# The preparation of an RWKV-7 recurrence put in a fixed order on three engines, its masks moved next to the Gram products, and Gram and bonus products merged into longer runs

## The chip, the cores and the metric

The kernel runs on one core of one Trainium2 chip. The core has five engines, each with its own queue of instructions that it works off strictly in the order in which they stand: TensorE (PE, matrix products and transposes into PSUM), VectorE (DVE), ScalarE (ACT), GpSimd (POOL) and SyncE (SP, which only issues DMA here; ACT issues some too). An instruction that has to wait holds up everything behind it in its own queue, and nothing else. The metric is the device time of one execution in microseconds.

## The reference

One layer of a decoder trunk over 1024 tokens of width 1024, in float32. Three branches read the same normalised input: an RWKV-7 recurrence, stick-breaking attention, and cross-attention into 256 memory tokens. They are gated, merged and projected; a feed-forward block with a causal convolution follows.

```python
h = rms_norm(x, norm1_g);  proj = h @ w_in
p_rwkv, p_sb, q_mem, gate_logits = split(proj)
# RWKV-7, 8 heads of 64
p = p + (shift(p) - p) * mu;  r, k, v, wl, al, gl = split(p)
decay = exp(-exp(-softplus(-(w0 + tanh(wl) @ w2)) - 0.5))
a = sigmoid(a0 + al @ a2);  g = sigmoid(gl) @ g2
kk = k * k_k;  kk = kk / max(norm(kk), 1e-12)       # per head
k = k * (1 + (a - 1) * k_a)
S_t = S * decay_t - (S kk_t) (kk_t a_t)^T + v_t k_t^T;   y_t = S_t r_t
y = (groupnorm(y) + bonus) * g,   bonus = sum(r * k * r_k) * v
# merge, then
x = x + sum_b(sigmoid(G_b) * (branch_b @ w_branch_b)) @ w_out
x = x + (silu(gate) * val) @ w_down,   gate, val = causal_conv3(rms_norm(x) @ w_up)
```

## The kernel before

Every large product is done as three products of rounded halves: a weight tile is loaded (`wr`), ACT copies it to a rounded high part (`wh`, L81), POOL subtracts to get the low part (`wl`, L82), and `mm3` issues high by high, high by low and low by high. A 1024-deep projection of 128 output columns and all 1024 tokens has eight steps of six matmuls over 512 tokens and fills two PSUM banks; the V projection of the stick-breaking attention (`sb_v`) fills four at once. PSUM has eight banks here: four of tag `mm` for projections, four of tag `g` for everything else.

The recurrence is computed in chunks of 64 tokens. `rwkv_prep(p, ...)`, called for p = 0 to 3 with two heads each, makes all that it needs: sigmoids of the low-rank products, the decay scan (L330), the norm of k by heads (`head_ss`, L333 to L337), the gate, the transposed v, kk and b (L369, L370), and for each half h of the tokens a pair of factors `bk`, `ra` (`chain(h)`, L379 to L382), their Gram products (`gram(h, f)`, f for a quarter: eight products of 128 by 128, then two masks L396 on DVE from PSUM to SBUF, then stores), a decayed copy on POOL (`decayed`, L408) and its transposes (`turned`). The bonus (L428 to L430) is made between chain(0) and gram(0).

`weave` interleaves that generator with `pump`, the stream of projections: after each `yield` of the preparation one step of the pump follows, six matmuls. So the PE order is written out by hand by the number of yields. While `self.pin` is set, `pinned` keeps PE's matmuls and transposes in program order; the instructions of the other engines are ordered by a scheduler from its own costs, with those in the preparation given priority (`high_priority`). A projection of the recurrence is finished by `shifted`: two products with a row scale (L246, which free the PSUM banks), a shifted copy on ACT (L247) and a final sum (L249). Behind the four preparations come the stick-breaking attention (`sb_attn`), the memory attention, `stage2` with the recurrence itself, and later the up phase and the down phase. Between them run on DVE the inverses of the triangular systems (L462, L464), driven by `pump`, and the differences of V rows (L681) which wait for loads of `vsd`.

In the down phase a step is 12 matmuls over one `draw` load: SP loads activations (`actd`, L1666) and weights (L1669), ACT copies both (L1676, L1677), DVE and POOL subtract (L1678, L1679). At the way into it the last tiles of the up phase are still convolved (L1473 on ACT, L1474, L1475 and L1481 on DVE) and combined (L1490), and ACT issues their stores to `actd` (L1495 to L1500).

## Time and profile before

| what | value |
| --- | --- |
| median of 3 runs | 1835.45 us (1835.12 to 1835.46) |
| the profiled execution | 1834.23 us |
| its span | 1832.5 us |
| mean clock granted to PE | 0.997 of full speed |
| preparations, about | 40 to 286 us |
| stick-breaking attention, about | 310 to 610 us |
| the way into the down phase | 1605 to 1630 us |

The span runs from the first to the last instruction of the profiled execution; its own time is a little longer, as it holds what lies around. In a waits view a row names the engine and line that waited, what released it, the total, the number and the longest wait in us. In a timeline a row has its start, its length, the line, the shapes, how many alike were joined (x), and in brackets the idle time before and what ended it. In a stretch of windows each engine has its busy time and, in brackets, its instructions, followed by the granted clock, the busy share of the DMA engines and their GB/s.

### The profile page before, as it was taken

The page shows a single profiled execution, that of the slowest core. Times are in us where ns is not written, and L with a number is a line of the kernel's source. Part 1 is how long each engine was busy: PE and PEld are TensorE (multiplying, and loading weights), DVE is VectorE, ACT ScalarE, POOL GpSimd, SP SyncE. Part 2 cuts the span into 40 slices and gives each one's busy share as a digit, 9 for nine tenths or more (in the row PEclk, how much of TensorE's full clock was granted, in tenths as well). Part 3 has the DMA queues.
Part 4 walks back from the last instruction along what each step waited for, and adds up shares of the span by engine and source line. Part 5 has one row for each costly group of instructions (what it writes and reads, how often), then busy time and mean ns, then how long its engine had stood idle before and what let it go on. Part 6 is the DMA issues. An engine that isn't in the chain of part 4 may idle for free.

```text
span 1832.5 us, 27438 instructions
## 1 busy us (share of the span) xinstructions
PE 1783.7 (97%) x10468; PEld 1442.8 (79%) x10468; DVE 1185.4 (65%) x1659; ACT 881.4 (48%) x1665; POOL 770.6 (42%) x441
## 2 busy tenths in 40 slices
PE   8999999999999999999899999989999999999999
PEld 6777778778788887787777878868888888878877
DVE  5657664988987514333534792597776777794596
ACT  5443342564666636534456533454444444444333
POOL 2322343232222452122233350476767767635454
PEclk9999999999999999999999999999999999999999
DMA  4155466111112342467665563323332323395475
GB/s 181 58 172 184 161 195 198 50 41 52 56 50 81 111 143 55 167 212 256 229 230 185 194 220 104 127 68 106 113 106 87 119 95 116 115 334 206 138 248 189
DMA packets 120614, 263.39 MB, mean 144 GB/s; under 512 B 28314, under 2 KB 40858, under 8 KB 120355
## 3 DMA queue, kind: packets, MB, share of 16 engines
q1 hardware_dynamic: 82722, 194.76, 32.3%
q10 hardware_dynamic: 33984, 54.27, 8.1%
q0 software_dynamic: 3776, 12.62, 2.2%
q8 instruction: 82, 1.34, 0.3%
q14 instruction: 50, 0.40, 0.1%
HBM read 180.04 MB, written 81.53 MB: 143 GB/s over the span
## 4 chain that ended last, share of the span: by engine, by line
PE 81%; DVE 10%; issue 4%; ACT 2%; POOL 2%; DMA 1%; ACTq 0%; SPq 0%; DVEq 0%; POOLq 0%
PE mm L113 65%; PE g L113 13%; PE g L106 3%; POOL dw L1679 1%; DVE at L854 1%; DVE it L462 1%; DVE qk L379 1%; DVE qk L381 1%; DVE inst L464 1%; DVE BT L1318 1%; DVE mg L1232 0%; DVE qk L817 0%; DMA at<-scr 0%; DVE g L1474 0%; ACT wh L81 0%
## 5 line engine op out<-in xcount | busy, mean ns | idle before, releaser
L82 POOL TENSOR_TENSOR wl<-wr,wh 128x1024 fp32r<-128x1024 f32 x77 | 196.5, 2552 | 475.0 <-ACT wh L81 464.1
L113 PE MATMUL mm<-xhi,wh 128*128 128x512 f32 x784 | 263.3, 416 | 10.1 <-ACT xhi L182 8.1
L113 PE MATMUL mm<-xlo,wh 128*128 128x512 f32 x784 | 244.7, 393 | 0.3 <-DVE xlo L183 0.3
L113 PE MATMUL mm<-xhi,wl 128*128 128x512 f32 x784 | 243.2, 392 | 0.7 <-POOL wl L82 0.7
L113 PEld LDWEIGHTS mm<-xhi,wl 128*128 128x128 f32 x784 | 147.6, 188 | 34.3 <-POOL wl L82 1.6
L113 PEld LDWEIGHTS mm<-xlo,wh 128*128 128x128 f32 x784 | 147.9, 189 | 33.8 <-DVE xlo L183 1.0
L113 PEld LDWEIGHTS mm<-xhi,wh 128*128 128x128 f32 x784 | 137.2, 190 | 40.1 <-issue 9.1
L81 ACT ACTIVATE wh<-wr 128x1024 fp32r<-128x1024 f32 x77 | 81.4, 1057 | 143.6 <-PE mm L113 87.3
L113 PE MATMUL mm<-dw,da 128*128 128x512 f32 x528 | 121.5, 390 | 2.2 <-DVE da L1678 2.0
L113 PEld LDWEIGHTS mm<-dw,da 128*128 128x128 f32 x528 | 98.8, 188 | 24.3 <-DVE da L1678 3.4
L113 PE MATMUL mm<-BT,l 128*128 128x512 f32 x504 | 117.7, 389 | 0.0
L1679 POOL TENSOR_TENSOR dw<-draw,dw 128x512 fp32r<-128x512 f32 x55 | 81.5, 1488 | 83.3 <-ACT dw L1677 83.2
L113 PE MATMUL mm<-BT,wh 128*128 128x512 f32 x352 | 109.2, 390 | 2.8 <-DVE BT L1318 2.8
L854 DVE TENSOR_TENSOR_SCAN at<-at,at 128x128 f32<-128x128 f32 (+3 forms) x64 | 93.3, 1459 | 26.6 <-ACT at L848 26.4
L113 PEld LDWEIGHTS mm<-BT,l 128*128 128x128 f32 x504 | 94.6, 188 | 19.6
L113 PE MATMUL mm<-B,wh 128*128 128x512 f32 x352 | 108.6, 390 | 1.5 <-DVE p L1508 1.5
L1678 DVE TENSOR_TENSOR da<-draw,da 128x512 fp32r<-128x512 f32 x77 | 65.7, 863 | 57.6 <-ACT da L1676 57.1
L113 PE MATMUL g<-dw,da 128*128 128x512 f32 x396 | 90.9, 390 | 2.1 <-POOL dw L1679 1.1
L1409 POOL TENSOR_TENSOR l<-it,l 128x1024 fp32r<-128x1024 f32 x21 | 51.6, 2459 | 95.5 <-ACT l L1408 95.5
L113 PEld LDWEIGHTS g<-dw,da 128*128 128x128 f32 x396 | 74.2, 188 | 18.3 <-ACT dw L1677 1.4
L1676 ACT ACTIVATE da<-draw 128x512 fp32r<-128x512 f32 x77 | 48.3, 629 | 83.6 <-PE mm L113 38.1
L756 DVE TENSOR_TENSOR w<-w,rbc 128x1024 f32<-128x1024 f32 x24 | 49.8, 2074 | 56.8 <-ACT w L755 55.0
(329 smaller groups left out, 3989.9 us busy)
## 6 DMA issues: line engine op xcount, KB each, us to landing
wr<-in_w_in_dram SPq DMA_DIRECT2D x50, 512.0 KB, 3.7
draw<-actd SPq DMA_DIRECT2D x77, 256.0 KB, 4.3
at<-scr SPq DMA_DIRECT2D x28, 512.0 KB, 6.1
draw<-in_w_down_dram SPq DMA_DIRECT2D x55, 256.0 KB, 4.9
rw<-in_w_up_dram SPq DMA_DIRECT2D x22, 512.0 KB, 3.5
actd<-gall ACTq DMA_DIRECT2D x44, 256.0 KB, 3.4
gsd<-w ACTq DMA_DIRECT2D x20, 512.0 KB, 2.8
wr<-in_w_up_dram SPq DMA_DIRECT2D x20, 512.0 KB, 3.7
```

The costliest lines, as they stand in the source:

```text
L81: self.nc.scalar.activation(hi, raw, AF.Copy)
L82: self.nc.gpsimd.tensor_tensor(lo, raw, hi.bitcast(F32), ALU.subtract)
L106: self.pinned(self.nc.tensor.transpose(out, in_, self.ident[:n, :n]))
L113: self.pinned(self.nc.tensor.matmul(*a, **k))
L379: nc.vector.tensor_tensor(bk4[q, :, first ^ h2], self.c8(x[q, hs]), self.c8(Q[q, hs]), ALU.mult)
L381: nc.vector.scalar_tensor_tensor(ra4[:, :, 1, 1:64], self.c8(P[:, hs])[:, :, 0:63], -1.0, self.c8(kk[:, hs])[:, :, 1:64], ALU.mult, ALU.mult)
L756: nc.vector.tensor_tensor(g, g, self.rbc, ALU.mult)
L854: self.pinned(nc.vector.tensor_tensor_scan(sn[:, :W][:, ::-1], sn[:, :W][:, ::-1], self.smask[:, 1024 - W :][:, ::-1], 1.0, ALU.mult, ALU. ...
L1409: keep(eng.tensor_tensor(lo, src, hi.bitcast(F32), ALU.subtract))
L1676: self.pinned(nc.scalar.activation(A[:, 0], a, AF.Copy))
L1678: self.pinned(nc.vector.tensor_tensor(A[:, 1], a, A[:, 0].bitcast(F32), ALU.subtract))
L1679: nc.gpsimd.tensor_tensor(Wt[:, 1], w, Wt[:, 0].bitcast(F32), ALU.subtract)
```

## The change

The number of instructions on each engine stays as it was, and what is computed too. Five things differ.

1. `pinned` now covers DVE, ACT and POOL instructions of the preparation, of `shifted` and, while `pin_split` is set, of the weight splits. It also adds an ordering dependency from each pinned instruction to the last one pinned on the same engine. That second part holds wherever `pin` is set, in the attention, the up phase and the down phase too.
2. The order inside a preparation: in `chain` the three `ra` instructions come ahead of the four `bk` ones; the bonus is made ahead of kk and b, right behind the transposes of v; the masks stand right behind their Gram products, ahead of chain(1).
3. The two `gram` calls of a half become one of 16 products with four banks, without pump steps between. The v transposes and the bonus products follow each other too.
4. The final sum of `shifted` is put off (`tails`) until the next projection's second step, or the first of `sb_v`.
5. A preparation has 31 yields where it had 27, and they stand elsewhere. Twelve steps of the pump move from behind the preparations into them.

```diff
 def split_raw(self, raw, hi, lo):
+    keep = self.pinned if self.pin_split else lambda ins: None
+    keep(self.nc.scalar.activation(hi, raw, AF.Copy))
+    keep(self.nc.gpsimd.tensor_tensor(lo, raw, hi.bitcast(F32), ALU.subtract))
...
 def pinned(self, ins):
     if self.pin:
         self.tc.keep_in_program_order(ins)
+        last = self.last_pinned.get(ins.ins.engine)
+        if last:
+            self.tc.add_manual_dep(
+                ins.ins, last, mybir.DependencyInfo(mybir.DependencyClass.NoSync, mybir.DependencyReason.DATA), reason="order")
+        self.last_pinned[ins.ins.engine] = ins.ins.name
+    return ins
...
 def shifted(self, ti, tag, pp=None):
...
+    finish = lambda: self.pinned(nc.vector.scalar_tensor_tensor(out, pr, self.omm[:, ti : ti + 1], tmp, ALU.mult, ALU.add))
+    if self.pin:
+        self.tails.append(finish)
+    else:
+        finish()
...
             self.mm3(pp, [a[:, ks] for a in w], self.xin(k), k == 0, k == 7)
+            if k == 1:
+                self.finish_tails()
...
 def rwkv_prep(self, p, krv, need):
...
+        for hs in halves:
+            pb = self.ps("g")
+            self.mmul(pb, self.blk, rk[:, hs], start=True, stop=True)
+            tt(bon[:, hs], pb, v[:, hs], ALU.mult)
...
         kk, b = k, a
         for hs, bc in zip(halves, self.bcast_heads(ex)):
+            stt(kk[:, hs], k[:, hs], self.par("k_k", p), bc, ALU.mult, ALU.mult)
+        tt(b, kk, a, ALU.mult)
...
-        def gram(h, f, bk, ra):
+        def gram(h, bk, ra):
+            pms = []
+            for f in range(2):
+                pm = [self.ps("g"), self.ps("g")]
+                for c in range(4):
+                    o = (f * 4 + c) * 128
+                    for h2 in range(2):
+                        q = slice(h2 * 64, h2 * 64 + 64)
+                        self.mmul(pm[h2][:, c * 128 : (c + 1) * 128], bk[q, o : o + 128], ra[q, o : o + 128], start=True, stop=True)
+                pms.append(pm)
+            for f, pm in enumerate(pms):
...
         u0 = chain(0)
         bp = decayed(0, u0[0])
...
-        gram(0, 0, *u0)
-        yield
-        gram(0, 1, *u0)
+        gram(0, *u0)
         u1 = chain(1)
-        for _ in range(2):
+        for _ in range(3):
             yield
         turned(0, bp)
         bp = decayed(1, u1[0])
-        for _ in range(4):
-            yield
-        gram(1, 0, *u1)
-        yield
-        gram(1, 1, *u1)
+        for _ in range(5):
+            yield
+        gram(1, *u1)
...
 def run(self):
+        self.pin_split = True
         for p in range(4):
             self.weave(self.rwkv_prep(p, krv[p], need), pump, 1.0)
+        self.pin_split = False
```

The rows below show how instructions stand in three places. A name like `at_1624<-g_1625` is the tile written and the tiles read; L332 and L333 of the changed kernel are its helpers for two-operand and three-operand DVE instructions.

First DVE in the third preparation, p = 2, before: from the second chain (`qk_1662`, `qk_1663`) to the masks of the first Gram products (`at_1624`, `at_1646`).

```order
L379 TENSOR_TENSOR qk_1662<-qk_1395,qk_1396 64x8x64 x2
L379 TENSOR_TENSOR qk_1662<-qk_1411,qk_1396 64x8x64 x2
L380 TENSOR_TENSOR qk_1663<-at_1214,qk_1409 128x8x64
L381 SCALAR_TENSOR_TENSOR qk_1663<-qk_1409,at_1099 128x8x63
L382 TENSOR_SCALAR qk_1663<-at_1099 128x8
L246 TENSOR_TENSOR w_249_1596<-mm_1492,rbc 128x512
L246 TENSOR_TENSOR w_249_1596<-mm_1493,rbc 128x512
L244 MEMSET w_270_1719 128x1
L249 SCALAR_TENSOR_TENSOR at_1602<-w_249_1596,omm,w_250_1597 128x1024
L396 TENSOR_TENSOR at_1624<-g_1625,kon 128x4x128
L396 TENSOR_TENSOR at_1624<-g_1626,kon 128x4x128
```

There the whole second chain and a shift with its final sum stand ahead of the first mask. The same place in the changed kernel, from kk (`at_1047`) and the first chain (`qk_1643`, `qk_1642`) on; `w_257_1660<-mm_1553` is the shift of the last projection of the recurrence, whose banks the V projection takes next:

```order
L333 SCALAR_TENSOR_TENSOR at_1047<-at_1047,params,g_1634 128x512
L332 TENSOR_TENSOR qk_1459<-at_1047,qk_1459 128x1024
L333 SCALAR_TENSOR_TENSOR qk_1643<-qk_1473,at_1047 128x8x63
L412 TENSOR_SCALAR qk_1643<-at_1047 128x8
L332 TENSOR_TENSOR qk_1643<-at_1173,qk_1473 128x8x64
L332 TENSOR_TENSOR qk_1642<-qk_1459,qk_1460 64x8x64 x2
L332 TENSOR_TENSOR qk_1642<-qk_1475,qk_1460 64x8x64 x2
L253 MEMSET w_258_1661 128x1
L255 TENSOR_TENSOR w_257_1660<-mm_1553,rbc 128x512
L255 TENSOR_TENSOR w_257_1660<-mm_1554,rbc 128x512
L258 SCALAR_TENSOR_TENSOR at_1666<-w_257_1660,omm,w_258_1661 128x1024
L332 TENSOR_TENSOR at_1740<-g_1720,kon 128x4x128
```

The mask (`at_1740`) now comes ahead of the second chain, and the shift behind the whole first one. In the changed kernel PE has between the second four head broadcasts (`g_1634`) and the product that needs the bank of `mm_1553` twelve matmuls.

Next ACT at the way into the down phase, before: the last convolution copies (`g`), the copies for the steps (`da`, `dw`; `draw_14208` is step 3's) and the stores to `actd`.

```order
L1473 ACTIVATE g_14136<-u_14067,params 128x512
L1676 ACTIVATE da_14211<-draw_14208 128x512
L1677 ACTIVATE dw_14212<-draw_14208 128x512
L1473 ACTIVATE g_14141<-u_14067,params 128x512
L1676 ACTIVATE da_14232<-draw_14229 128x512
L1495 DMA actd<-gall 128x512 x2
L1677 ACTIVATE dw_14233<-draw_14229 128x512
```

And in the changed kernel:

```order
L1498 ACTIVATE g_14136<-u_14067,params 128x512
L1498 ACTIVATE g_14141<-u_14067,params 128x512
L1520 DMA actd<-gall 128x512 x3
L1525 DMA actd<-gall 128x3x512
L1524 DMA actd<-gall 128x512
L1701 ACTIVATE da_14211<-draw_14208 128x512
L1702 ACTIVATE dw_14212<-draw_14208 128x512
```

All five stores now stand ahead of the copies for step 3. On SP the loads of step 3 stand in the changed kernel behind the loads of four later steps and two loads of `u` (before: behind neither of these):

```order
L1691 DMA draw_14257<-actd 128x512
L1694 DMA draw_14257<-in_w_down_dram 128x512
L1691 DMA draw_14278<-actd 128x512
L1694 DMA draw_14278<-in_w_down_dram 128x512
L1691 DMA draw_14327<-actd 128x512
L1694 DMA draw_14327<-in_w_down_dram 128x512
L1677 DMA u_14250<-in_w_down_dram 128x1024
L1691 DMA draw_14355<-actd 128x512
L1694 DMA draw_14355<-in_w_down_dram 128x512
L1677 DMA u_14299<-in_w_down_dram 128x1024
L1691 DMA draw_14208<-actd 128x512
L1694 DMA draw_14208<-in_w_down_dram 128x512
```

`u_14299` takes the buffer that the last convolution products read, so it and all behind it start only when DVE has finished these.

More of the change, by code (lines that the diff above doesn't have):

```diff
@@ L54, in __init__ @@
         self.uid = 0
-        self.pin = False
+        self.pin = self.pin_split = False
+        self.tails = []
+        self.last_pinned = {}
     def nm(self, s):
@@ L80, in split_raw @@
     def split_raw(self, raw, hi, lo):
-        self.nc.scalar.activation(hi, raw, AF.Copy)
-        self.nc.gpsimd.tensor_tensor(lo, raw, hi.bitcast(F32), ALU.subtract)
+        keep = self.pinned if self.pin_split else lambda ins: None
+        keep(self.nc.scalar.activation(hi, raw, AF.Copy))
+        keep(self.nc.gpsimd.tensor_tensor(lo, raw, hi.bitcast(F32), ALU.subtract))
         return hi, lo
@@ L243, in shifted, with finish_tails @@
         pr, tmp = self.t4(), self.t4()
-        nc.vector.memset(tmp[:, 0:1], 0.0)
+        self.pinned(nc.vector.memset(tmp[:, 0:1], 0.0))
         for h in range(2):
-            nc.vector.tensor_tensor(pr[:, h * 512 : (h + 1) * 512], pp[h], self.rbc[:, h * 512 : (h + 1) * 512], ALU.mult)
-        nc.scalar.activation(tmp[:, 1:1024], pr[:, 0:1023], AF.Copy, scale=self.par("mu", ti))
+            self.pinned(nc.vector.tensor_tensor(pr[:, h * 512 : (h + 1) * 512], pp[h], self.rbc[:, h * 512 : (h + 1) * 512], ALU.mult))
+        self.pinned(nc.scalar.activation(tmp[:, 1:1024], pr[:, 0:1023], AF.Copy, scale=self.par("mu", ti)))
         out = self.t4(tag)
-        nc.vector.scalar_tensor_tensor(out, pr, self.omm[:, ti : ti + 1], tmp, ALU.mult, ALU.add)
-        return out
+        finish = lambda: self.pinned(nc.vector.scalar_tensor_tensor(out, pr, self.omm[:, ti : ti + 1], tmp, ALU.mult, ALU.add))
[3 more added lines that the diff above has]
+            finish()
+        return out
+    def finish_tails(self):
+        while self.tails:
+            self.tails.pop(0)()
     def expand_heads(self, f, tag="w4"):
@@ L254, in expand_heads @@
         ex = self.t4(tag)
-        nc.vector.tensor_copy(
+        ins = nc.vector.tensor_copy(
             ex[:, :1024].rearrange("p (j h i) -> p j h i", j=8, h=2),
@@ L258, in expand_heads @@
         )
+        if tag == "it":
+            self.pinned(ins)
         return ex
@@ L309, in rwkv_prep @@
         halves = [slice(0, 512), slice(512, 1024)]
+        act = lambda *a, **k: self.pinned(nc.scalar.activation(*a, **k))
+        tt = lambda *a: self.pinned(nc.vector.tensor_tensor(*a))
+        stt = lambda *a: self.pinned(nc.vector.scalar_tensor_tensor(*a))
         if p == 0:
@@ L319, in rwkv_prep @@
             self.mmul(pu, lora[0:64, cs], wa[0:64, hs], start=True, stop=True)
-            nc.scalar.activation(a[:, hs], pa, AF.Sigmoid, bias=self.par("a0", p))
-            nc.scalar.activation(su[:, hs], pu, AF.Sigmoid, bias=self.par("w0", p))
+            act(a[:, hs], pa, AF.Sigmoid, bias=self.par("a0", p))
+            act(su[:, hs], pu, AF.Sigmoid, bias=self.par("w0", p))
         P = self.t4("qk")
-        nc.scalar.activation(P, k, AF.Square, scale=self.par("k_k", p))
+        act(P, k, AF.Square, scale=self.par("k_k", p))
         kp = self.t4("qk")
-        nc.scalar.activation(kp, a, AF.Identity, scale=self.par("k_a", p), bias=self.omka[:, p : p + 1])
-        nc.vector.tensor_tensor(kp, k, kp, ALU.mult)
+        act(kp, a, AF.Identity, scale=self.par("k_a", p), bias=self.omka[:, p : p + 1])
         for _ in range(2):
@@ L329, in rwkv_prep @@
         cc = Q = su
-        nc.vector.tensor_tensor_scan(cc, self.seg, su, 0.0, ALU.mult, ALU.add)
+        self.pinned(nc.vector.tensor_tensor_scan(cc, self.seg, su, 0.0, ALU.mult, ALU.add))
+        tt(kp, k, kp, ALU.mult)
         for _ in range(2):
@@ L334, in rwkv_prep @@
         mx = self.small("rs", [128, 16])
-        nc.vector.tensor_scalar(mx, pst, 1e-24, None, ALU.max)
+        self.pinned(nc.vector.tensor_scalar(mx, pst, 1e-24, None, ALU.max))
         inv = self.small("inv", [128, 16])
-        nc.gpsimd.tensor_tensor(inv, mx, self.half[:, :16], ALU.pow)
+        self.pinned(nc.gpsimd.tensor_tensor(inv, mx, self.half[:, :16], ALU.pow))
         g = self.t4("qk")
@@ L341, in rwkv_prep @@
             self.mmul(pgh, lora[:, 512 + p * 128 : 512 + (p + 1) * 128], self.sg[:, hs], start=True, stop=True)
-            nc.scalar.activation(g[:, hs], pgh, AF.Copy)
-        nc.scalar.activation(P, cc, AF.Exp, scale=-EXPM, bias=self.offs[:, 0:1])
+            act(g[:, hs], pgh, AF.Copy)
+        act(P, cc, AF.Exp, scale=-EXPM, bias=self.offs[:, 0:1])
         pc = self.pc[p]
-        nc.scalar.activation(pc, cc.rearrange("p (c s) -> p c s", c=NC)[:, :, 63], AF.Exp, scale=-EXPM)
-        nc.scalar.activation(Q, cc, AF.Exp, scale=EXPM, bias=self.offs[:, 1:2])
-        ex = self.expand_heads(inv, "it")
+        act(pc, cc.rearrange("p (c s) -> p c s", c=NC)[:, :, 63], AF.Exp, scale=-EXPM)
+        act(Q, cc, AF.Exp, scale=EXPM, bias=self.offs[:, 1:2])
         for _ in range(3):
             yield
+        ex = self.expand_heads(inv, "it")
         need(f"v{p}")
@@ L352, in rwkv_prep @@
         rk = self.t4("qk")
-        nc.vector.scalar_tensor_tensor(rk, r, self.par("r_k", p), kp, ALU.mult, ALU.mult)
+        stt(rk, r, self.par("r_k", p), kp, ALU.mult, ALU.mult)
+        yield
+        yield
         vt = self.t4("qk")
+        bon = v
         for h, hs in enumerate(halves):
@@ L358, in rwkv_prep @@
                 self.transpose(pt[:, j * 128 : (j + 1) * 128], v[:, (h * 4 + j) * 128 : (h * 4 + j + 1) * 128])
-            nc.scalar.activation(vt[:, hs], pt, AF.Copy)
+            act(vt[:, hs], pt, AF.Copy)
+        for hs in halves:
+            pb = self.ps("g")
+            self.mmul(pb, self.blk, rk[:, hs], start=True, stop=True)
+            tt(bon[:, hs], pb, v[:, hs], ALU.mult)
         for c2 in range(2):
@@ L364, in rwkv_prep @@
                     vt[c2 * 64 : c2 * 64 + 64].rearrange("s (g h i) -> s g h i", g=NG, h=2)[:, :, h2])
-        for _ in range(2):
+        stt(bon, bon, self.par("lnx_b", p), g, ALU.add, ALU.mult)
+        act(g, g, AF.Copy, scale=self.par("lnx_g", p))
+        nc.sync.dma_start(self.ggd[p, 1], bon)
+        nc.scalar.dma_start(self.ggd[p, 0], g)
+        for _ in range(3):
             yield
@@ L368, in rwkv_prep @@
         for hs, bc in zip(halves, self.bcast_heads(ex)):
-            nc.vector.scalar_tensor_tensor(kk[:, hs], k[:, hs], self.par("k_k", p), bc, ALU.mult, ALU.mult)
-        nc.vector.tensor_tensor(b, kk, a, ALU.mult)
+            stt(kk[:, hs], k[:, hs], self.par("k_k", p), bc, ALU.mult, ALU.mult)
+        tt(b, kk, a, ALU.mult)
         def chain(h):
@@ L375, in chain @@
             bk4, ra4 = (x.rearrange("p (c u s) -> p c u s", c=8, u=2) for x in (bk, ra))
+            stt(ra4[:, :, 1, 1:64], self.c8(P[:, hs])[:, :, 0:63], -1.0, self.c8(kk[:, hs])[:, :, 1:64], ALU.mult, ALU.mult)
+            self.pinned(nc.vector.tensor_scalar(ra4[:, :, 1, 0], self.c8(kk[:, hs])[:, :, 0], -math.exp(OFF), None, ALU.mult))
+            tt(ra4[:, :, 0], self.c8(r[:, hs]), self.c8(P[:, hs]), ALU.mult)
             for x, first in ((b, 1), (kp, 0)):
@@ L378, in chain @@
                     q = slice(h2 * 64, h2 * 64 + 64)
-                    nc.vector.tensor_tensor(bk4[q, :, first ^ h2], self.c8(x[q, hs]), self.c8(Q[q, hs]), ALU.mult)
-            nc.vector.tensor_tensor(ra4[:, :, 0], self.c8(r[:, hs]), self.c8(P[:, hs]), ALU.mult)
-            nc.vector.scalar_tensor_tensor(ra4[:, :, 1, 1:64], self.c8(P[:, hs])[:, :, 0:63], -1.0, self.c8(kk[:, hs])[:, :, 1:64], ALU.mult, ALU.mult)
-            nc.vector.tensor_scalar(ra4[:, :, 1, 0], self.c8(kk[:, hs])[:, :, 0], -math.exp(OFF), None, ALU.mult)
+                    tt(bk4[q, :, first ^ h2], self.c8(x[q, hs]), self.c8(Q[q, hs]), ALU.mult)
@@ L383, in chain @@
             self.spill(p, h, 0, ra, nc.sync)
             return bk, ra
-        def gram(h, f, bk, ra):
-            mt = self.t4("at")
-            mt4 = mt.rearrange("p (c h t) -> p c h t", c=4, h=2)
-            pm = [self.ps("g"), self.ps("g")]
-            for c in range(4):
-                o = (f * 4 + c) * 128
-                for h2 in range(2):
-                    q = slice(h2 * 64, h2 * 64 + 64)
-                    self.mmul(pm[h2][:, c * 128 : (c + 1) * 128], bk[q, o : o + 128], ra[q, o : o + 128], start=True, stop=True)
-            for h2 in range(2):
-                nc.vector.tensor_tensor(
-                    mt4[:, :, h2], pm[h2].rearrange("p (c t) -> p c t", c=4),
-                    self.mm_mask.unsqueeze(1).to_broadcast([128, 4, 128]), ALU.mult)
-            g0 = h * 4 + f * 2
-            nc.sync.dma_start(
-                self.scr[p, g0 : g0 + 2, :, 512:1024].rearrange("g q c -> q g c"), mt.rearrange("q (g c) -> q g c", g=2))
-            for h2 in range(2):
-                i0 = p * 32 + h2 * 16 + h * 8 + f * 4
-                nc.sync.dma_start(self.mad[i0 : i0 + 4].rearrange("c s t -> s c t"), mt4[64 - h2 * 64 : 128 - h2 * 64, :, h2, 64:128])
+        def gram(h, bk, ra):
[9 more added lines that the diff above has]
+            for f, pm in enumerate(pms):
+                mt = self.t4("at")
+                mt4 = mt.rearrange("p (c h t) -> p c h t", c=4, h=2)
+                for h2 in range(2):
+                    tt(mt4[:, :, h2], pm[h2].rearrange("p (c t) -> p c t", c=4),
+                       self.mm_mask.unsqueeze(1).to_broadcast([128, 4, 128]), ALU.mult)
+                g0 = h * 4 + f * 2
+                nc.sync.dma_start(
+                    self.scr[p, g0 : g0 + 2, :, 512:1024].rearrange("g q c -> q g c"), mt.rearrange("q (g c) -> q g c", g=2))
+                for h2 in range(2):
+                    i0 = p * 32 + h2 * 16 + h * 8 + f * 4
+                    nc.sync.dma_start(self.mad[i0 : i0 + 4].rearrange("c s t -> s c t"), mt4[64 - h2 * 64 : 128 - h2 * 64, :, h2, 64:128])
@@ L406, in decayed @@
         def decayed(h, bk):
             bp = self.t4("it")
-            nc.gpsimd.tensor_tensor(
-                self.c8(bp), self.c8(bk), pc[:, h * 8 : h * 8 + 8].unsqueeze(2).to_broadcast([128, 8, 128]), ALU.mult)
+            self.pinned(nc.gpsimd.tensor_tensor(
+                self.c8(bp), self.c8(bk), pc[:, h * 8 : h * 8 + 8].unsqueeze(2).to_broadcast([128, 8, 128]), ALU.mult))
             return bp
@@ L417, in turned @@
                     self.transpose(pt[:, c * 128 : (c + 1) * 128], bp[:, (f * 4 + c) * 128 : (f * 4 + c + 1) * 128])
-                nc.scalar.activation(bt[:, f * 512 : (f + 1) * 512], pt, AF.Copy)
+                act(bt[:, f * 512 : (f + 1) * 512], pt, AF.Copy)
             self.spill(p, h, 256, bt, nc.scalar)
@@ L422, in rwkv_prep @@
         bp = decayed(0, u0[0])
-        for _ in range(2):
+        for _ in range(7):
             yield
-        bon = v
-        for hs in halves:
-            pb = self.ps("g")
-            self.mmul(pb, self.blk, rk[:, hs], start=True, stop=True)
-            nc.vector.tensor_tensor(bon[:, hs], pb, v[:, hs], ALU.mult)
-        nc.vector.scalar_tensor_tensor(bon, bon, self.par("lnx_b", p), g, ALU.add, ALU.mult)
-        nc.sync.dma_start(self.ggd[p, 1], bon)
-        nc.scalar.activation(g, g, AF.Copy, scale=self.par("lnx_g", p))
-        nc.scalar.dma_start(self.ggd[p, 0], g)
-        for _ in range(4):
-            yield
-        gram(0, 0, *u0)
-        yield
-        gram(0, 1, *u0)
+        gram(0, *u0)
         u1 = chain(1)
-        for _ in range(2):
+        for _ in range(3):
             yield
@@ L443, in rwkv_prep @@
         bp = decayed(1, u1[0])
-        for _ in range(4):
+        for _ in range(5):
             yield
-        gram(1, 0, *u1)
-        yield
-        gram(1, 1, *u1)
+        gram(1, *u1)
         for _ in range(3):
@@ L665, in item @@
                         self.raw.append(raw)
+                if i == 0:
+                    self.finish_tails()
                 if i == 1:
```

## The prediction

> **What bounds the kernel now.** I read the page's busy line and chain of waits first, then the waits of PE (TensorE) by stretch, then PE's own timeline around each wait.

> ```profile
> span 1832.5 us, 27438 instructions
> PE 1783.7 (97%) x10468; PEld 1442.8 (79%) x10468; DVE 1185.4 (65%) x1659; ACT 881.4 (48%) x1665; POOL 770.6 (42%) x441
> PE 81%; DVE 10%; issue 4%; ACT 2%; POOL 2%; DMA 1%; ACTq 0%; SPq 0%; DVEq 0%; POOLq 0%
> ```

> PE is busy 97% of 1832.5 us, and the chain runs 81% on it. No matmul is added or removed here, so the change can only move the 49 us in which PE stands still, and the clock at which it runs. What stands still in the four preparations shows in PE's waits from 40 to 310 us (total, number, longest):

> ```profile
> PE g L106 <- DVE at L396: 6.4, 3, 2.6
> PE g L113 <- DVE qk L382: 2.4, 2, 1.8
> ...
> PE g L106 <- DVE at L249: 0.4, 1, 0.4
> ```

> The two first rows are what the change aims at: PE wants a PSUM bank that a mask (L396) has not yet read out, or a factor (L382) that DVE (VectorE) has not yet written. With the L249 row they are 9.2 us. PE's timeline gives the price of each run and of the clock (start, length, line, count, idle before):

> ```profile
> 103.55 1.16 PE L106 MATMUL g<-kon,it 128*128 128x128 f32 x8 [2.26 <-DVE at L396]
> ...
> 205.14 1.16 PE L113 MATMUL g<-qk,qk 64*128 64x128 f32 x16 [0.67 <-DVE qk L382]
> 206.23 0.74 PE L113 MATMUL mm<-xhi,wh 128*128 128x512 f32 x2
> ...
> 207.84 1.16 PE L113 MATMUL g<-qk,qk 64*128 64x128 f32 x16
> ...
> 213.54 1.16 PE L106 MATMUL g<-kon,it 128*128 128x128 f32 x8 [1.56 <-DVE at L396]
> 214.46 0.71 PE L113 MATMUL mm<-xhi,wh 128*128 128x512 f32 x2
> 215.01 0.62 PE L113 MATMUL mm<-xlo,wh 128*128 128x512 f32 x2
> ...
> 217.73 0.62 PE L113 MATMUL mm<-xlo,wh 128*128 128x512 f32 x2
> ...
> 269.14 1.97 PE L106 MATMUL g<-kon,it 128*128 128x128 f32 x8 [2.57 <-DVE at L396]
> ...
> 272.51 0.40 PE L113 MATMUL mm<-wh,xlo 128*128 128x512 f32 x1
> ```

> From 215.01 to 217.73 stand 12 projection matmuls: 2.72 us, 0.227 each. The eight transposes take 1.16 us at 103.55 and 213.54, but 1.97 at 269.14. That is the clock: the window from 240 to 280 us was granted 0.96 of full speed.

> ```profile
> 240.00:280.00 40.00, 37.43 (x195) 28.88 (x195) 27.77 (x27) 13.49 (x19) 21.39 (x9) 0.96 0.70 227
> 400.00:500.00 100.00, 96.54 (x667) 78.65 (x667) 92.08 (x77) 56.50 (x106) 27.06 (x11) 1.00 0.15 48
> ```

> Columns are PE, weight loads, DVE, ACT (ScalarE), POOL (GpSimd), clock, DMA. From 269.14 to 272.51, 3.37 us, PE does eight transposes and four matmuls; at full clock the transposes hold PE for 214.46 - 213.54 = 0.92 and the matmuls for 0.91, 1.83 in all. So a wait of 2.57 us was followed by about 1.5 us of lost clock, one of 2.26 by none.

> **What is removed.** (1) The 9.2 us of waits: masks stand right behind their products and ahead of the second chain(), and the shift's last step no longer stands between. (2) The halved clock behind the 2.57 us wait: 1.5. (3) Two halves of a Gram group were parted by six matmuls. These took from 206.23 to 207.84 = 1.61 us, where six by 0.227 are 1.36; merging saves 0.25 in each of eight groups, 2.0. Together -12.7 us.

> [...]

> **What is added in the third preparation.** These are DVE's prices (shortest/median/longest ns, 40 to 300 us):

> ```profile
> L379 DVE TENSOR_TENSOR qk<-qk,qk x32: 669/686/691, 78.9 to 263.1; 64x512 f32<-64x512 f32 x32
> L380 DVE TENSOR_TENSOR qk<-at,qk x8: 691/693/2284, 89.6 to 263.8; 128x512 f32<-128x512 f32 x8
> L381 DVE SCALAR_TENSOR_TENSOR qk<-qk,at x8: 671/1364/2874, 90.8 to 264.4; 128x504 f32<-128x504 f32 x8
> L382 DVE TENSOR_SCALAR qk<-at x8: 160/164/2359, 93.6 to 267.2; 128x8 f32<-128x8 f32 x8
> L369 DVE SCALAR_TENSOR_TENSOR at<-at,params,g x8: 739/744/749, 84.2 to 249.9; 128x512 f32<-128x512 f32 x8
> L370 DVE TENSOR_TENSOR qk<-at,qk x4: 1224/1224/1224, 85.7 to 250.7; 128x1024 f32<-128x1024 f32 x4
> L246 DVE TENSOR_TENSOR w<-mm,rbc x26: 673/680/693, 46.4 to 219.2; 128x512 f32<-128x512 f32 x26
> ```

> In p = 2 the last shifted projection ends where the V projection of stick-breaking attention begins, which takes four PSUM banks at once. Its third bank is free when the shift's product (L246) has read it. In the new order that product stands behind the whole kk, b and chain(0), which begin only when PE has made the second four head broadcasts: 0.74 + 1.22 + 0.67 + 0.16 + 0.69 + 4 x 0.69 + its own 0.68 = 6.9 us. PE has 12 matmuls as cover, 2.7. So it waits 4.2 us where it waited 0. If the cover were gone it would be 6.9. The L381 row's median is 1.36 rather than 0.67 and its longest 2.87, so up to 6 us is possible; below, 3 if a matmul run more lies between. I take 4.2, by the shortest rows, since POOL has no split then. ACT's and POOL's next weight split follow late; PE meets that with some 0.5 more. A wait of 4.2 is longer than the 2.57 that cost clock: +1.5. In p = 0 and 1 the following projection needs two banks, and they are free. Sum: +6.2.

> **The fourth preparation and the inverse.**

> ```profile
> 264.40 2.87 DVE L381 SCALAR_TENSOR_TENSOR qk<-qk,at 128x504 f32<-128x504 f32 x1
> ...
> 267.27 1.21 DVE L681 TENSOR_TENSOR A<-A,w 128x1024 f32<-128x1024 f32 x1
> 268.41 2.47 DVE L396 TENSOR_TENSOR at<-g,kon 128x512 f32<-128x512 f32 x4
> ```

> ```profile
> DVE A L681 <- DMA A<-vsd: 23.4, 3, 10.4
> ```

> The differences of V (L681) wait for a load, 23.4 us in three waits, and still stand ahead of masks of p = 3. That they now come a little earlier for PE costs between 0 and 4; I take 1, since the loads are issued no later. Twelve pump steps of six matmuls, 72 x 0.227 = 16.3 us of PE, move from behind the preparations into them. This alone moves no end. But the triangular inverse (L462, L464) then starts later against PE, inside the attention stage where DVE is busy 92 of 100 us. I take +1.5 (with the POOL order ahead of it), between -2 and +5: bounds are nothing, and a third of the 16.3.

> **What is added at the way into the down phase.** The new rule chains every pinned instruction, here too. In the new order SP issues the loads of step 3 behind a `u` load which waits for the last convolution product (L1475), and ACT copies them behind five stores of `actd` which wait for DVE's L1490.

> ```profile
> 1612.96 1.29 PE L113 MATMUL mm<-dw,da 128*128 128x512 f32 x5
> ```

> ```profile
> 1628.89 1.43 PE L113 MATMUL mm<-dw,da 128*128 128x512 f32 x5 [1.35 <-DVE da L1678]
> ```

> ```profile
> 1609.39 0.38 SPq L1666 DMA_DIRECT2D draw<-actd  x1
> ...
> 1615.41 0.33 SPq L1652 DMA_DIRECT2D u<-in_w_down_dram  x1
> ```

> ```profile
> 1617.77 1.41 DVE L1475 SCALAR_TENSOR_TENSOR g<-u,params,g 128x512 f32<-128x512 f32 x2
> 1619.09 1.28 DVE L1481 TENSOR_TENSOR gall<-g,gall 128x512 f32<-128x512 f32 x2
> ...
> 1622.84 2.98 DVE L1490 TENSOR_TENSOR gall<-gall 128x512 f32<-128x512 f32 x3
> ```

> ```profile
> draw<-actd SPq DMA_DIRECT2D x77, 256.0 KB, 4.3
> ...
> draw<-in_w_down_dram SPq DMA_DIRECT2D x55, 256.0 KB, 4.9
> ```

> ```profile
> 1614.06 0.63 ACT L1676 ACTIVATE da<-draw 128x512 fp32r<-128x512 f32 x1 [0.70 <-DMA draw<-actd]
> ```

> ```profile
> L1679 POOL TENSOR_TENSOR dw<-draw,dw x12: 1287/1294/1576, 1598.7 to 1638.2; 128x512 fp32r<-128x512 f32 x12
> ```

> A step is 12 matmuls, 2.72 us. PE begins at 1612.96, so step 3 is due at 1612.96 + 8.16 = 1621.1. L1475 ends at 1619.2; the weight half of the step's load then goes out at about 1619.9 instead of about 1609.8, lands 4.9 later at 1624.8, is copied (0.63) and split by POOL (1.29): ready at 1626.7. PE waits 5.6 us. The old wait of 1.35 behind it goes, as DVE catches up in the meantime: net +4.2. This is longer than 2.57 too: +1.5 of clock. Bounds: 0, if the `u` load gets its buffer earlier, and +8 if the load lands 2 us late among the others. I take +5.7.

> **The sum.** -12.7 + 6.2 + 1 + 1.5 + 5.7 = +1.7. The profiled execution took 1834.23 us (span 1832.5), 1.2 below the median of 1835.45, so the difference is put on the median: **1837 us**. Its own range is 1833 to 1841.

> **Rivals.** *The new waits are short (faster).* The 12.7 us rest on rows that exist; the two new waits are worked out from an order. If one of them is covered (the down phase by a `u` buffer that is free sooner, or the bank in p = 2), 5.7 to 6.2 us fall away: 1831; if both, 1825. Against it: in both places a named instruction stands ahead in the same queue. Chance 0.27.

> *DVE becomes the bound in the attention stage (slower).* Place: 310 to 610 us, where it has 8 of 100 us free. With the inverse 16.3 us later against PE it would need that slack for what it did before the stage. From the point at which its work passes 100 of 100, what PE gained ahead is given back there: up to 12.7 less the 1.5 already counted, and without the 2.0 of runs that stay saved, +9: 1846. For it: in that row PE stands still for 3.5 of 100 us already. Against: DVE's total is the same. Chance 0.15.

> *The waits of the preparations do not go, they move (slower).* DVE has as many instructions in each preparation; in a fixed order each wait for a load or a bank holds all behind it. Then the 9.2 stay in other places: 1846. Against: DVE is busy only 65% of the span, and an order that sets readers behind their products leaves less standing in front of them. Chance 0.10.

> **How the numbers follow.** The forecast has 0.45, these rivals 0.27, 0.15 and 0.10, and 0.03 are left. A measurement of this kernel can tell 0.2%, 3.7 us: 1831.8 to 1839.1. Faster: 0.26 of the first rival, 0.02 of the forecast, 0.01 left over, 0.29. Same: 0.30 of the forecast, 0.01 of the first rival and 0.02 of the others, 0.33. Slower: the rest, 0.38. The range reaches from the middle of the first rival to the times of the two others: 1826 to 1847, which leaves about 2 in 10 out.

> **What would show it.** Right, step by step: no wait of PE for masks over 0.5 us before 180 us; products of 32 records in one run; a wait for the shift's product of about 4 us near the start of the V projection, behind it transposes or matmuls at half clock; a wait of 5 to 6 us in the fourth step of the down phase, for POOL's `dw` or DVE's `da`. Wrong: masks still waited for in p = 0 and 1; no wait at the V projection (then the faster rival); waits for L462 or for attention's scan growing by more than 4 us (then DVE is the bound).

## The result, and the profile after

The changed kernel took 1865.11 us, the median of four runs from 1864.79 to 1865.92, against 1835.45 us before (1835.12 to 1836.35). The ratio is 1.0156, with an interval of 1.0144 to 1.0168: slower by 29.7 us, where the forecast was 1837 and the range ended at 1847. The page of the changed kernel (same columns as before):

```profile
span 1863.4 us, 27452 instructions
PE 1793.3 (96%) x10468; PEld 1451.1 (78%) x10468; DVE 1176.5 (63%) x1659; ACT 882.4 (47%) x1665; POOL 779.4 (42%) x441
PEclk9899999999999999999999999999999999989999
PE 68%; DVE 7%; issue 3%; DMA 2%; ACT 1%; POOL 1%; SPq 0%; POOLq 0%; DVEq 0%; ACTq 0%
```

PE has the same 10468 matmuls. It is busy 9.6 us longer for them, which is clock: the mean granted clock is 0.986 where it was 0.997, and its row has two slices at 8 of 10 where there was none. The other 21 us of the span it stands still. Since the two kernels run as many matmuls, and in the same order from the end of the preparations on, the start of the n-th matmul in one trace can be set against the n-th in the other. This is worked out from the two traces; a change in the last column is time that PE lost or won between two rows.

```
n       before    after     after - before
0          8.1      7.5       -0.6
200       51.3     65.1      +13.8
1000     197.1    206.2       +9.0
1200     235.2    254.8      +19.6
1600     308.6    324.1      +15.5
3800     633.2    646.5      +13.3
4400     718.6    732.0      +13.4
4600     753.5    777.5      +24.0
5600     886.1    907.0      +21.0
9400    1580.0   1600.7      +20.6
9600    1626.0   1657.8      +31.8
10400   1813.1   1844.1      +30.9
```

Four jumps are to be explained: 14.4 us ahead of the first preparation, 10.6 in the third, 10.6 in the memory attention and 11.1 at the way into the down phase. Three stretches won: 4.8 in the first two preparations, 6.3 behind the third (n = 1200 to 3800) and 3.0 near 890 us (n = 4600 to 5600). PE's waits in the changed kernel from 40 to 310 us, and then from 700 to 1000, stand against those at L396, L382 and L249 of the kernel before:

```profile
PE mm L122 <- ACT wh L84: 10.9, 1, 10.9
PE g L122 <- DVE qk L333: 5.6, 2, 3.1
PE mm L122 <- DVE w L255: 4.4, 1, 4.4
PE mm L122 <- POOL wl L85: 0.5, 1, 0.5
PE g L109 <- DVE at L332: 0.4, 1, 0.4
```

```profile
PE mm L122 <- DVE qk L1062: 4.3, 1, 4.3
PE g L122 <- ACT at L1098: 3.8, 1, 3.8
PE g L122 <- DVE ys L553: 2.0, 1, 2.0
PE g L122 <- ACT qk L573: 1.4, 1, 1.4
```

The masks (L332 at) are down from 6.4 to 0.4 us, so the change does what it says. But in the same 270 us there is a wait for a weight split on ACT of 10.9 us, and three more for DVE. PE's timeline has each with what follows it:

```profile
57.17 1.22 PE L122 MATMUL mm<-xhi,wh 128*128 128x512 f32 x2 [10.89 <-ACT wh L84]
...
230.65 0.79 PE L122 MATMUL mm<-wh,xhi 128*128 128x512 f32 x1 [4.40 <-DVE w L255]
...
1649.84 0.79 PE L122 MATMUL mm<-dw,da 128*128 128x512 f32 x1 [7.91 <-ACT dw L1702]
```

And the windows behind them (PE, weight loads, DVE, ACT, POOL, clock, DMA):

```profile
57.00:61.00 4.00, 3.30 (x7) 2.20 (x8) 0.49 (x1) 1.06 (x2) 3.75 (x2) 0.50 0.12 11
61.00:65.00 4.00, 4.00 (x10) 3.09 (x10) 0.00 (x0) 0.00 (x0) 1.05 (x1) 0.50 0.73 243
...
230.60:234.60 4.00, 3.95 (x9) 3.14 (x10) 1.87 (x2) 2.09 (x2) 2.42 (x2) 0.50 0.00 0
234.60:238.60 4.00, 4.00 (x16) 3.24 (x15) 0.00 (x0) 1.06 (x1) 1.48 (x2) 0.84 0.33 111
...
1649.80:1653.80 4.00, 3.40 (x7) 2.41 (x8) 3.42 (x3) 3.11 (x6) 3.93 (x3) 0.50 0.32 130
1653.80:1657.80 4.00, 4.00 (x14) 3.13 (x14) 4.00 (x4) 1.15 (x2) 2.83 (x3) 0.75 0.85 220
```

After these three waits PE ran at half clock for 8.0, 5.2 and 6.0 us, up to 65.20, 235.87 and 1655.81; between n = 9400 and 9600, where the wait of 7.91 us lies, it lost 11.1 us. What stands ahead of the late split at the start shows in ACT's timeline of the changed kernel:

```profile
47.26 1.15 ACT L256 ACTIVATE w<-w,params 128x1023 f32<-128x1023 f32 x1 [4.39 <-DVE w L253]
49.76 1.06 ACT L223 ACTIVATE A<-A 64x1024 f32<-64x1024 f32 x1 [1.35 <-DVE A L258]
51.14 1.15 ACT L256 ACTIVATE w<-w,params 128x1023 f32<-128x1023 f32 x1 [0.33 <-DVE w L253]
52.31 1.28 ACT L225 ACT_TABLE_LOAD   x1
53.64 1.06 ACT L225 ACTIVATE A<-A 128x1024 f32<-128x1024 f32 x1
55.02 1.15 ACT L256 ACTIVATE w<-w,params 128x1023 f32<-128x1023 f32 x1 [0.33 <-DVE w L253]
56.08 1.99 ACT L84 ACTIVATE wh<-wr 128x1024 fp32r<-128x1024 f32 x2
```

Two weight splits (L84) stand behind three shifts, two other activations and a table load, which wait for DVE in turn. Before, the same two splits began at 43.59 and 45.00 us, ahead of all of these. `pin_split` had made program order binding for them, and in program order they come last.

### The profile page after: what moved, and what is told of

Read it like the earlier page. It is cut to its first block, busy times and chain, and to the rows that moved or that the text cites. A ratio compares the mean times of both kernels' runs of the same rounds, so it can differ in the third digit from the quotient of the medians.

```text
span 1863.4 us, 27452 instructions
## 1 busy us (share of the span) xinstructions
PE 1793.3 (96%) x10468; PEld 1451.1 (78%) x10468; DVE 1176.5 (63%) x1659; ACT 882.4 (47%) x1665; POOL 779.4 (42%) x441
## 4 chain that ended last, share of the span: by engine, by line
PE 68%; DVE 7%; issue 3%; DMA 2%; ACT 1%; POOL 1%; SPq 0%; POOLq 0%; DVEq 0%; ACTq 0%
PE mm L122 56%; PE g L122 10%; PE g L109 3%; DVE mg L1257 1%; POOL dw L1704 1%; DVE at L879 1%; DVE at L1250 1%; DVE BT L1343 0%; DVE inst L487 0%; DMA w<-mrd 0%; DVE it L485 0%; DMA mrd<-w 0%; DMA w<-yd 0%; DMA actd<-gall 0%; DVE at L1245 0%
## 5 line engine op out<-in xcount | busy, mean ns | idle before, releaser
L122 PE MATMUL mm<-xhi,wh 128*128 128x512 f32 x784 | 264.7, 418 | 19.8 <-ACT wh L84 10.9
L84 ACT ACTIVATE wh<-wr 128x1024 fp32r<-128x1024 f32 x77 | 81.2, 1055 | 107.4 <-PE mm L122 56.2
L879 DVE TENSOR_TENSOR_SCAN at<-at,at 128x128 f32<-128x128 f32 (+3 forms) x64 | 86.4, 1352 | 20.6 <-ACT at L873 20.4
## 6 DMA issues: line engine op xcount, KB each, us to landing
draw<-actd SPq DMA_DIRECT2D x77, 256.0 KB, 3.2
draw<-in_w_down_dram SPq DMA_DIRECT2D x55, 256.0 KB, 4.6
actd<-gall ACTq DMA_DIRECT2D x44, 256.0 KB, 3.3
```

The lines of the kernel that those rows point to most:

```text
L84: keep(self.nc.scalar.activation(hi, raw, AF.Copy))
L122: self.pinned(self.nc.tensor.matmul(*a, **k))
L879: self.pinned(nc.vector.tensor_tensor_scan(sn[:, :W][:, ::-1], sn[:, :W][:, ::-1], self.smask[:, 1024 - W :][:, ::-1], 1.0, ALU.mult, ALU. ...
```

## The experiments

On the chip of the first four runs the kernel before had a median of 1836.9 us; in the second group 1836.9, in the third 1837.07. Ratios are to it.

### The dependency alone

```diff
         last = self.last_pinned.get(ins.ins.engine)
-        if last:
+        if False:
```

> The changed kernel without the added dependency from each pinned instruction to the last one; the pinning itself stays. Its orders inside the four preparations are the same as with it, outside they are those of the kernel before. Theory D (the dependency alone makes the losses of 10.5 us around 730 to 780 us and of about 10 us at the way into the down phase): both go, with the 3.0 us that the changed kernel gains near 890 us: 1865.1 - 10.5 + 3.0 - 9.5 = about 1848. Rival I (these losses come from the inverse that the new preparations start later, so that its results arrive late): the loss around 750 us stays, only the down phase is mended: about 1855.

Measured: 1860.89 us, ratio 1.0128 (1.0112 to 1.0144). The wait at the way into the down phase is 1.4 us again. The stretch from n = 4400 to 4600 kept its jump (+10.5 against the kernel before), and the 3 us near 890 us were not won. So theory D holds for the down phase and falls for the memory attention. The time lies above both expected values; with the 10.5 us left in, the sum of the expectation would have been about 1859. Rival I put the loss that stays down to late results of the inverse; what makes it is shown further down. The dependency has nothing to do with the order inside the preparations: without it every engine's order there is the same, since the pinning alone sets it.

### The weight splits free in the first preparation

```diff
-        self.pin_split = True
         for p in range(4):
+            self.pin_split = p > 0
             self.weave(self.rwkv_prep(p, krv[p], need), pump, 1.0)
```

> The changed kernel with the weight splits pinned only from the second preparation on, the dependency kept. Theory S (the 14 us before the first preparation are two pinned ACT splits that stand behind three shifts, a table load and a copy): PE's wait of 10.9 us for ACT goes, and the half clock behind it: 1865.1 - 14 = about 1851. Rival W (the splits are late because their weight loads or buffers are late): the wait stays, 1863 to 1866.

Measured: 1851.26 us, ratio 1.0077 (1.006 to 1.0094). The 10.9 us wait is gone and the 200th matmul starts at 50.6 us where it started at 51.3 before: 14 us, theory S.

### Both

> Both of these edits in one kernel. If the losses are apart in time and add up: 1848 + 1851 - 1865 = about 1834, no change against the kernel before; the waits of the third preparation (4.4 us for the shift's product, 3.1 us for the bonus factor) should still be there. If the startup's delay hid others behind it: 1838 or more.

Measured: 1845.46 us, ratio 1.0043 (1.0024 to 1.0061), and 1839.8 in the span of the profiled run. This is 12 us more than foreseen by its median; the memory attention's 11 us, which the expectation still gave to the dependency, are the difference. At the end of the preparations (n = 1600) PE is 0.5 us ahead of the kernel before. It was 5.0 ahead at n = 1000, lost 10.7 in the third preparation and won 6.2 behind it: most of what the masks and merges win is lost in the third.

### The memory attention's splits

In that stage the exponentials (L1098) are pinned and the weight splits are not. ACT in the kernel above, where PE waits 4.3 us for L1062:

```profile
723.37 1.06 ACT L84 ACTIVATE wh<-wr 128x1024 fp32r<-128x1024 f32 x1 [6.70 <-PE mm L122]
724.34 0.54 ACT L1098 ACTIVATE at<-g,nb,hf 128x256 f32<-128x256 f32 x1
```

The split waits 6.70 us for a buffer which PE still reads, and four exponentials wait behind it, though all they need is there from 719.9 us on; PE then waits for what they make. In the kernel before this split stood behind them.

```diff
+        self.pin_split = True
         self.weave(self.mem_attn(mq, need), pump, 1.6, 0)
+        self.pin_split = False
```

> The kernel without the dependency and with splits pinned from p = 1, and in the memory attention the weight splits pinned too. There ACT's split stood ahead of four exponentials and waited 6.7 us for a buffer that PE frees; pinned, it stands behind them. Theory A (this place in ACT's queue makes the two waits of 4.3 and 3.8 us near 730 to 770 us and the clock behind them): the 11 us of that stretch go, 1845.5 - 11 = about 1834. Rival I (late results of the inverse or of the loads make them): the stretch keeps its 11 us, 1842 to 1847.

Measured: 1833.42 us, ratio 0.9984 (0.9972 to 0.9995). In the profile the split stands behind the exponentials, and PE's wait at that place is 0.47 us; the second, for L1098, is 1.1 instead of 3.8:

```profile
727.89 1.98 PE L122 MATMUL mm<-at,A 128*128 128x512 f32 x4 [0.47 <-DVE qk L1062]
```

Between n = 4400 and 4600 PE loses nothing (-0.7 against +11.4). Theory A; the edit also moves stores and other instructions on POOL's queue and loads on SP's, so the split is not the only thing that moved. Why the scheduler put that one split elsewhere when only the preparations had changed was not tried; it did so in every kernel with the new preparations and free splits there.

### The third and fourth preparation, mended in two steps

In DVE's timeline of the changed kernel ahead of the wait for the bonus factor (L333, at 214.87):

```profile
209.49 1.28 DVE L258 SCALAR_TENSOR_TENSOR at<-w,omm,w 128x1024 f32<-128x1024 f32 x1 [2.99 <-ACT w L256]
210.69 2.84 DVE L272 COPY it<-inv 128x1024 f32<-128x1024 f32 x1
213.45 1.27 DVE L333 SCALAR_TENSOR_TENSOR qk<-at,params,qk 128x1024 f32<-128x1024 f32 x1
```

The factor waits behind an expansion that takes 2.84 us instead of 0.69 while POOL's split runs (210.48 to 212.98; the last section has more on this), and that behind a final sum which waits for ACT. The second wait is that for the bank, as forecast.

```diff
-        ex = self.expand_heads(inv, "it")
         stt(rk, r, self.par("r_k", p), kp, ALU.mult, ALU.mult)
+        ex = self.expand_heads(inv, "it")
...
+        yield
         u0 = chain(0)
         bp = decayed(0, u0[0])
-        for _ in range(7):
+        for _ in range(6):
             yield
```

> Both edits, and two more inside the preparation: one of the seven yields behind chain(0) comes ahead of it, so that the last shift's product which frees a PSUM bank for the V projection stands ahead of chain(0) on DVE; and the bonus factor r k r_k comes ahead of the expansion of the norms. Theory P (the two waits of the third and the one of the fourth preparation come from these two places in DVE's queue): 4.4 + 3.1 + 2.5 us of waits go and some 4 us of half clock: about 1823. Rival M (a fixed order only moves them, to the Gram products or the masks): 1830 to 1836.

Measured: 1842.88 us, ratio 1.0031 (1.002 to 1.0041), on the kernel with both edits and without the memory attention's: 2.6 us less than that, not 11. The bank's wait is gone (0.2) and so is that of the fourth preparation for its bonus factor; that of the third is still 2.5 us instead of 3.1, and a new one stands right behind the bank's place:

```profile
210.49 0.50 PE L122 MATMUL mm<-wh,xhi 128*128 128x512 f32 x1 [0.20 <-DVE w L255]
220.43 0.80 PE L122 MATMUL mm<-wl,xhi 128*128 128x512 f32 x1 [5.09 <-POOL wl L85]
```

```profile
215.18 2.90 POOL L446 TENSOR_TENSOR it<-qk,pc 128x1024 f32<-128x1024 f32 x1 [15.78 <-DVE qk L332]
218.04 4.66 POOL L85 TENSOR_TENSOR wl<-wr,wh 128x1024 fp32r<-128x1024 f32 x2
```

POOL had been idle for 15.78 us, waiting for chain(0) so as to make the decayed copy (L446), while the split that stands behind it had its input from ACT at 213.2. Rival M, in this place: a fixed order only handed the wait on. The next kernel, `all_mended`, puts the decayed copy four yields later, gives the bonus factor one yield more, and has the memory attention's edit too.

```diff
         u0 = chain(0)
+        for _ in range(4):
+            yield
         bp = decayed(0, u0[0])
-        for _ in range(6):
+        for _ in range(2):
             yield
```

> The same, and in the preparations: a yield between b and chain(0), the bonus factor ahead of the expansion of the norms and one more yield between it and the transposes of v, and the decayed copy four yields later, so that on POOL the weight split, ready before it, stands ahead. Theory P (what is left are places in queues): waits of the third and fourth preparation under 2 us, and the shift of PE against the kernel before at the end of the preparations -9 to -12 us instead of 0: about 1824, faster than before. Rival M (a fixed order only moves the waits): another wait of 3 to 6 us in the third or fourth preparation, 1832 to 1836.

Measured: 1824.35 us (1824.02 to 1824.7), ratio 0.9928 (0.9913 to 0.9942): 12.5 us faster than the kernel before, and the version that beats both. Its waits from 55 to 310 us:

```profile
PE mm L122 <- POOL wl L85: 1.5, 2, 0.9
PE g L122 <- DVE qk L333: 1.1, 1, 1.1
PE g L122 <- DVE qk L332: 0.8, 2, 0.6
PE mm L122 <- DVE w L255: 0.2, 1, 0.2
```

3.6 us in all, none over 1.1, and PE is 11.1 us ahead of the kernel before at n = 1600, 0.8 of which is there from the first matmul on.

### The merge by itself, and taken out

```diff
-        gram(0, 0, *u0)
-        yield
-        gram(0, 1, *u0)
+        yield
+        gram(0, *u0)
```

(and for the second half alike, in the kernel before)

> The kernel before with one edit: the two Gram calls of a half merged into 16 products, the pump step that stood between them ahead of both; order of the other engines left to the scheduler. Theory (each of the eight merges saves 0.25 us of PE's entry into another kind of product, and no more): -2 us, 1835 against 1837, if the masks of four banks do not make the transposes wait longer. Rival (all four g banks are taken at once and the next product waits for the masks): waits for L396 grow by 1 to 3 us each, 1840 or more.

Measured for this kernel, `merge_alone`: 1841.7 us, ratio 1.0026 (1.0017 to 1.0036), 4.8 us more than the kernel before. PE's waits from 40 to 310 us:

```profile
PE g L106 <- DVE at L400: 14.0, 4, 5.5
PE mm L113 <- DVE w L246: 0.5, 1, 0.5
PE g L113 <- DVE qk L382: 0.4, 1, 0.4
PE g L106 <- DVE at L249: 0.4, 1, 0.4
```

The waits for masks (L400 here) went from 6.4 to 14.0 us: all four `g` banks are full after 16 products, and while the masks stand behind chain(1) and a shift in DVE's queue, the transposes that come next have no bank. The other direction takes the merge out of the mended kernel:

> all_mended with the Gram products in two halves again, six pump matmuls and the masks of the first half between them; the yields behind are one fewer, so that PE has the same work. Theory (a merge saves 0.25 us of PE in each of eight groups where no mask is waited for): 1824.4 + 2 = 1826 to 1827. Rival (with the masks right behind their products the merge takes four banks at once and costs as much as it saves): 1824, no difference.

Measured: 1828.7 us (1826.81 to 1829.81), ratio 0.9955 (0.9938 to 0.9972) to the kernel before, 4.3 us more than `all_mended` had in the group before. PE's n-th matmul is 4.3 us later at the end of the preparations; 0.7 of this is there before the first preparation (n = 50), and the other 3.6 come in eight nearly equal steps, one with each group of products. None of its waits in the preparations is longer. So with masks next to the products a merge is worth some 0.45 us for each of the eight, nearly twice what was forecast; without them it costs. What makes a step 0.45 rather than 0.25 was not followed.

### The dependency back in the mended kernel

> all_mended with the added dependency back; orders in the preparations and the attention stage are the same, the way into the down phase is as in the changed kernel. Theory D (the dependency costs what PE lost there, about 9.5 us, and gives back the 3 us near 890 us): 1824.4 + 9.5 - 3 = about 1831. Rival (the 9.5 us came with the later arrival of the phase, not with the order): 1822 to 1825.

Measured: 1832.78 us, ratio 0.9979 (0.997 to 0.9989), 8.4 us more than `all_mended`. The wait is 9.5 us, though the phase starts 30 us earlier than in the changed kernel:

```profile
1619.01 0.80 PE L122 MATMUL mm<-dw,da 128*128 128x512 f32 x1 [9.50 <-ACT dw L1707]
```

PE lost 13.3 us between n = 9400 and 9600. It had won 3.5 between n = 5400 and 5600 and lost 2.3 of that again by n = 5800. Theory D; the 3 us near 890 us are given back only in part.

## Why the prediction was wrong

**What was removed** held in the main. The three items were put at 12.7 us; the mended kernel, where nothing takes them back, is 11.1 us ahead at the end of the preparations with 3.6 us of waits left. The merges were mis-sized: 0.25 each as forecast, some 0.45 as measured.

**The first step that failed** is a term that the sum does not have: it adds nothing for what is ahead of the third preparation. Of p = 0 and 1 the prediction says only that the next projection's banks are free, and the pinned weight splits count in it only as 0.5 us in the third. But two of them were moved behind the shifts ahead of the first preparation, from 43.59 and 45.00 to 56.08 us, and cost 14.4 us, half of the whole miss. The prediction does not walk ACT's queue there.

**The second is the memory attention**, 10.6 us, which has no term in the sum at all. With the first it makes 25 of the 28 us between forecast and result. It was not touched by the diff; one free split stood ahead of four exponentials in ACT's queue. The split, placed ahead of them, passed its own wait of 6.70 us on to them, and not only its own 1.06 us: the exponentials could have begun at 719.9 and began at 724.34, 4.4 us later, and PE's first wait there is 4.3.

**The third preparation** was right in mechanism and in size for the bank: 4.2 forecast, 4.40 measured. The clock behind it was put at 1.5 us; the two windows behind 230.60 us, at 0.50 and 0.84 of full speed, make it 2.6. The wait for the bonus factor was missed (3.1 us, and 2.5 in the fourth): the sum has no term for it. In DVE's queue the factor stands behind a final sum that waits for ACT and an expansion of 2.84 us instead of 0.69, and neither was walked.

**The fourth preparation and the inverse** were put at +2.5 and gave some time back: from n = 1200 to 3800 PE won 6.3 us. The traces also have 90 more matmuls of the projections ahead of the last transposes of the fourth preparation, which is fifteen steps of the pump and not twelve: 20.4 us of PE, not 16.3. The rival that DVE becomes the bound in the attention stage did not come. The rival that the waits only move came in part: not for the masks, but the waits for the bonus factor, the bank and the split on ACT are new ones behind a fixed order.

**The down phase** was right in place and mechanism, and the size was off: 5.6 us forecast as the wait, 7.91 measured, and 1.5 us of clock, measured at some 2.7 (11.1 lost between n = 9400 and 9600, less the waits of 7.91 and 0.56). A missing piece is in SP's queue:

```profile
1639.90 0.33 SPq L1677 DMA_DIRECT2D u<-in_w_down_dram  x1
1643.00 0.33 SPq L1691 DMA_DIRECT2D draw<-actd  x1
```

```profile
SPq L1691 <- DMA actd<-gall: 2.8, 1, 2.8
```

Behind the load of `u`, which went out when foreseen, the load of step 3 stood 2.8 us longer. It waits for a store to `actd` that ACT issued between 1636.63 and 1640.78 us, a wait that the sum did not have.

**The clock.** In the changed kernel it fell, from 40 us on, with each of PE's five waits of 3.79 us and more (0.50 to 0.62 of full speed in the 4 us behind them), but also with waits of 3.13 us (214.80 to 218.80 at 0.57) and 2.46 us (283.40 to 287.40, 0.57 as well). It did not fall with one of 2.71 us in `merge_alone` (103.60 to 107.60 at 1.00):

```profile
103.68 1.17 PE L106 MATMUL g<-kon,it 128*128 128x128 f32 x8 [2.71 <-DVE at L400]
```

```profile
265.54:268.95 3.41, 1.04 (x5) 0.53 (x3) 3.41 (x4) 0.00 (x0) 1.19 (x1) 1.00 0.84 327
268.96:272.37 3.41, 3.23 (x12) 2.94 (x13) 1.92 (x4) 2.25 (x3) 2.16 (x1) 0.50 0.89 269
```

```profile
99.43:102.84 3.41, 1.54 (x7) 0.94 (x5) 2.20 (x5) 1.15 (x1) 0.00 (x0) 1.00 0.80 304
102.85:106.26 3.41, 2.58 (x15) 2.22 (x16) 2.69 (x6) 1.40 (x3) 1.28 (x1) 1.00 0.34 117
```

So the length of a wait alone did not give its price in clock here. That it also counts where the wait lies against these windows is the author's estimate from the rows above; no run moved a wait to show it.

## What to carry to other kernels

An order that is made binding for a queue binds everything in it: walk each queue from its first pinned instruction, also those ahead of the loop that one means to change, and ask of every instruction that moved forward what it waits for. After such a change, set the n-th matmul of one trace against the n-th of the other before reading any wait: it says in one table where the time went, and that the stage edited was not where most of it was lost. Merging runs of products and draining their banks at once belonged together here: the eight merges won 3.6 us in the preparations with the masks next to the products, and the kernel with the merges alone took 4.8 us more. Each is worth measuring with the other in place.

## What the runs showed that was not expected

DVE took longer beside a split on POOL, also on an operation that reads one tile: the expansion L272 took from 694 to 2862 ns over the four preparations of the changed kernel, 0.69 us at 85.58 and 148.32 us with no split beside it, and 2.84 and 2.86 at 210.69 and 279.20 beside one. The bonus factor, which reads two, took 3.40 us in `all_mended` where a split ran beside it, and 1.27 at 213.45 us in the changed kernel where none did.

```profile
L272 DVE COPY it<-inv x4: 694/1768/2862, 85.6 to 279.2; 128x1024 f32<-128x1024 f32 x4
```

```profile
195.99 3.40 DVE L333 SCALAR_TENSOR_TENSOR qk<-at,params,qk 128x1024 f32<-128x1024 f32 x1
```

```profile
195.78 2.53 POOL L85 TENSOR_TENSOR wl<-wr,wh 128x1024 fp32r<-128x1024 f32 x1 [5.14 <-ACT wh L84]
```

The ends tell more than the lengths. The factor ended at 199.39 us, 1.08 behind the split (198.31); the expansion at 210.69 us in the changed kernel ended at 213.53, 0.55 behind its split (212.98), and the one at 279.20 again 0.55 behind. Both distances are a little under the instruction's own time without a split beside it, 1.27 and 0.69. In these three cases the time fits an instruction on DVE that stands until the split is nearly done and then runs at its usual speed better than one that runs more slowly throughout; this is the author's estimate from the ends, and no run was made to show which it is.
